# A decoder layer on one core: the second MLP product in seven half-depth products, with operand sums made by transfers, and a reordered SSD loop

## The chip, the cores and the metric

The kernel runs as one program on 1 core of a Trainium2 chip. Its metric is the device time of one execution in microseconds. Matrix products run on TensorE (PE; PEld is its weight load), element work on VectorE (DVE), ScalarE (ACT) and GpSimd (POOL). SyncE (SP), ACT and POOL also issue transfers (DMA) between DRAM and the on-chip memory SBUF; products are accumulated in PSUM banks.

## What is computed

One layer on 1024 tokens of width 1024, in float32: a norm, a wide input projection, three mixers side by side (GLA, windowed attention, Mamba-2 SSD), a gated merge, an output projection, and then the MLP. The two places that the change touches are, cut from the reference:

```python
def _ssd(z, xbc, dt_raw, ...):                       # 32 heads in 4 groups, chunks of 128 tokens
    a_cs = jnp.cumsum(dtc * A, axis=2)
    seg = a_cs[:, :, :, None] - a_cs[:, :, None, :]
    Lmat = jnp.exp(jnp.where(causal, seg, -inf))     # decay between two tokens of a chunk, per head
    CB = jnp.einsum('bnlgd,bnsgd->bnlsg', Cc, Bc)
    y_diag = jnp.einsum('bnlsgh,bnsghp->bnlghp', CB[..., None] * Lmat, xdt)
    ...                                              # plus the state carried from chunk to chunk
    y = (y_diag + y_off + D_skip * xc) * silu(z)     # then a norm over the 512 columns of a group

h2 = _rmsnorm(x, norm_mlp)
x = x + (jnp.square(jax.nn.relu(h2 @ w_mlp_in)) @ w_mlp_out) * vmask     # 1024 -> 4096 -> 1024
return _rmsnorm(x, final_norm)
```

## The kernel before

Every float32 operand of a large product is split into a high part `hi` (a ScalarE cast) and a rest `lo` (a VectorE subtraction), and a product is three matmuls: hi by hi, hi by lo, lo by hi. The first part of the kernel holds the normed input in SBUF and makes the projection beside the mixers; work that no mixer waits for (the `z` and gate projections, lines 158 to 160 and 186 to 188) is put between the mixers' steps to fill TensorE. The order of the instructions on each engine is made when the program is built, from priorities (`tc.high_priority`) and the scheduler's own idea of durations; at run time each engine takes its list in order, and an instruction that waits holds up all behind it on its engine.

**SSD (lines 557 to 673).** For each of 4 groups, 8 chunks c of 128 tokens. A transfer from SP (L632) spreads the chunk's running sums of 8 heads over all partitions into the 128x1024 tile `ab` (two buffers), another (L634) loads `zt`. POOL subtracts the per-token sums (L635), DVE clamps at 0 (L636), ACT takes the exponential (L637), DVE multiplies by `cb` (L638). Eight small matmuls, one per head, give `psD` (L643), one gives `psY` from the carried state (L646), one the next state (L657). DVE and POOL assemble y (L648 to L662), ACT sums its squares into `zt` (L664), POOL makes the reciprocal root by a power (L88), ACT scales y (L666), and TensorE transposes y in four pieces at once (L669), followed by a copy (L671) and a store. So the transposes of a chunk stand in TensorE's list before the next chunk's `psD` or close to it.

**MLP.** The first product already runs as seven products per unit of 256 hidden columns (`unit_a` to `unit_e`, 16 units); a unit leaves four 128x512 tiles of the squared ReLU in DRAM (`hid_d`), named here by K half and token half: x11, x21, x12, x22. The second product (lines 1039 to 1080) runs over 16 blocks of 256 rows of K: two loads of hidden values and two of weights (512 KB each, from SP), splits (L152, L153 and L127, L128), then for 8 token tiles and 2 column halves six matmuls of 512 columns (L847 to L849) and one addition into the residual `x2b` (L1062). In the last block the final norm and the output stores follow each token tile. Pools that matter: 22 tiles `o` of 128x1024 float32 (split operands), 2 pairs `w_hi`, `w_lo`, 3 tiles `w_raw`, 4 tiles `h2`, 8 PSUM banks.

## Time and profile before

| | us |
|---|---|
| median of 3 runs (2729.49 to 2734.89) | 2734.1 |
| the profiled execution's own time | 2735.99 |
| its span in the trace | 2734.4 |
| SSD loops of the four groups, in the span | 954 to 1025, 1134 to 1212, 1335 to 1408, 1515 to 1589 |
| second MLP product, in the span | 2371 to 2724 |

The profile is of one execution. A row of a group gives the line of the code, the engine, the operation with output and input tiles, how often it ran, then the busy time in us and the mean of one in ns, and after the second bar the idle time of the engine just before it and what ended that. "PEclk" is the share of full speed that TensorE's clock was granted. A matmul on float32 (not split) operands is recorded twice.

### The profile page before, as it was taken

To read this page: it belongs to the slowest core of one execution; us is meant where nothing else is said; L and a number is where in the kernel's file an instruction comes from. 1 tells how busy PE (TensorE), PEld (TensorE's weight loads), DVE (VectorE), ACT (ScalarE), POOL (GpSimd) and SP (SyncE) were. 2 spreads that over 40 slices of the span, in tenths; PEclk is the share of its full clock that TensorE was granted. 3 is DMA by queue.
4 is the path that set the end of the run, shared out by engine and by line. 5 is a ranking of instruction groups with operands and counts; after the bars stand their busy time and mean duration, and the time that the engine had idled before them with its cause. 6 is when DMAs were issued, how large, how long until landed. Compare 5 with 4: busy or idle time off the path is not lost.

```text
span 2734.4 us, 36866 instructions
## 1 busy us (share of the span) xinstructions
PE 2634.5 (96%) x14565; PEld 2284.4 (84%) x14565; DVE 1451.0 (53%) x2463; ACT 1049.2 (38%) x1915; POOL 386.2 (14%) x326
## 2 busy tenths in 40 slices
PE   8999999999999989989989899999998999999998
PEld 7998988888888979879879678888996888888887
DVE  5333323256664573653655653444437666676666
ACT  6423433246664454353454343323234333321212
POOL 1000000011221150340340410322200000000001
PEclk9999999999999999989989999999998999999999
DMA  4211112212223152252251464433322333533231
GB/s 141 63 40 54 47 47 62 77 52 76 61 68 93 51 123 74 67 122 74 76 133 46 122 224 150 150 113 110 124 78 81 108 108 113 204 124 96 93 100 62
DMA packets 223951, 260.48 MB, mean 95 GB/s; under 512 B 14382, under 2 KB 176484, under 8 KB 223780
## 3 DMA queue, kind: packets, MB, share of 16 engines
q1 hardware_dynamic: 178820, 207.74, 25.7%
q10 hardware_dynamic: 44960, 50.40, 5.2%
q8 instruction: 114, 1.87, 0.3%
q14 instruction: 57, 0.47, 0.1%
HBM read 195.05 MB, written 63.05 MB: 94 GB/s over the span
## 4 chain that ended last, share of the span: by engine, by line
PE 80%; DVE 5%; DMA 5%; ACT 4%; issue 3%; POOL 2%; SPq 0%; ACTq 0%; POOLq 0%; DVEq 0%
PE acc_ps L158 8%; PE acc_ps L159 8%; PE acc_ps L160 8%; PE pp_ps L778 8%; PE pp_ps L849 5%; PE pp_ps L847 5%; PE pp_ps L848 5%; PE pp_ps L781 4%; DMA ab<-acs_d 4%; PE pp_ps L933 3%; PE pp_ps L935 3%; PE pp_ps L936 3%; PE acc_ps L186 3%; PE acc_ps L188 3%; PE acc_ps L187 3%
## 5 line engine op out<-in xcount | busy, mean ns | idle before, releaser
L158 PE MATMUL acc_ps<-hh,w_hi 128*128 128x512 f32 (+6 forms) x1320 | 472.0, 358 | 3.3 <-ACT rt L352 1.7
L159 PE MATMUL acc_ps<-hl,w_hi 128*128 128x512 f32 (+6 forms) x1320 | 475.1, 360 | 0.0
L160 PE MATMUL acc_ps<-hh,w_lo 128*128 128x512 f32 (+6 forms) x1320 | 470.6, 356 | 0.0
L186 PE MATMUL acc_ps<-w_hi,hh 128*128 128x256 f32 x1056 | 308.4, 292 | 1.9 <-ACT zst L199 1.3
L187 PE MATMUL acc_ps<-w_lo,hh 128*128 128x256 f32 x1056 | 309.0, 293 | 0.0
L188 PE MATMUL acc_ps<-w_hi,hl 128*128 128x256 f32 x1056 | 308.1, 293 | 0.0
L128 DVE TENSOR_TENSOR w_lo<-w_raw,w_hi 128x1024 fp32r<-128x1024 f32 (+1 forms) x156 | 200.5, 1307 | 155.4 <-ACT w_hi L127 155.3
L158 PEld LDWEIGHTS acc_ps<-hh,w_hi 128*128 128x128 f32 (+1 forms) x1320 | 247.6, 188 | 32.8 <-ACT rt L352 2.6
L847 PE MATMUL pp_ps<-w_hi,o 128*128 128x512 f32 (+1 forms) x768 | 270.7, 354 | 1.4 <-ACT w_hi L127 1.4
L849 PE MATMUL pp_ps<-w_hi,o 128*128 128x512 f32 (+1 forms) x768 | 271.5, 354 | 0.1
L848 PE MATMUL pp_ps<-w_lo,o 128*128 128x512 f32 (+1 forms) x768 | 271.4, 354 | 0.0
L159 PEld LDWEIGHTS acc_ps<-hl,w_hi 128*128 128x128 f32 (+1 forms) x1320 | 247.8, 188 | 26.6 <-issue 2.4
L160 PEld LDWEIGHTS acc_ps<-hh,w_lo 128*128 128x128 f32 (+1 forms) x1320 | 248.0, 188 | 26.0 <-issue 2.4
L127 ACT CAST w_hi<-w_raw 128x1024 fp32r<-128x1024 f32 (+1 forms) x156 | 154.7, 1040 | 274.7 <-PE pp_ps L849 122.2
L188 PEld LDWEIGHTS acc_ps<-w_hi,hl 128*128 128x128 f32 x1056 | 201.3, 191 | 11.2 <-issue 10.5
L186 PEld LDWEIGHTS acc_ps<-w_hi,hh 128*128 128x128 f32 x1056 | 201.6, 191 | 9.2 <-issue 4.7
L187 PEld LDWEIGHTS acc_ps<-w_lo,hh 128*128 128x128 f32 x1056 | 201.3, 191 | 5.3 <-issue 4.4
L781 PE MATMUL pp_ps<-o,w_hi 128*128 128x512 f32 x512 | 198.9, 389 | 0.0
L778 PE MATMUL pp_ps<-o,w_hi 128*128 128x512 f32 x512 | 197.1, 389 | 1.2 <-ACT o L152 1.2
L1062 DVE TENSOR_TENSOR x2b<-pp_ps,x2b 128x512 f32<-128x512 f32 x256 | 169.3, 685 | 45.4 <-PE pp_ps L849 43.5
L933 PE MATMUL pp_ps<-o,w_hi 128*128 128x512 f32 x448 | 177.4, 398 | 9.3 <-ACT o L152 9.2
L935 PE MATMUL pp_ps<-o,w_hi 128*128 128x512 f32 x448 | 177.2, 395 | 2.1 <-DVE o L153 2.1
(298 smaller groups left out, 4657.1 us busy)
## 6 DMA issues: line engine op xcount, KB each, us to landing
w_raw<-in_w_in_dram SPq DMA_DIRECT2D x80, 512.0 KB, 3.7
ab<-acs_d SPq DMA_DIRECT2D x32, 512.0 KB, 9.2
g<-gate SPq DMA_DIRECT2D x64, 256.0 KB, 4.0
w_raw<-in_w_mlp_in_dram SPq DMA_DIRECT2D x32, 512.0 KB, 4.1
hid<-hid ACTq DMA_DIRECT2D x64, 256.0 KB, 3.3
w_raw<-hid SPq DMA_DIRECT2D x32, 512.0 KB, 4.4
w_raw<-in_w_mlp_out_dram SPq DMA_DIRECT2D x32, 512.0 KB
gate<-gst ACTq DMA_DIRECT2D x48, 256.0 KB, 2.0
```

The source lines that it names most:

```text
L158: nc.tensor.matmul(ps, lhsT=lh, rhs=rh, start=(i == 0), stop=False)
L159: nc.tensor.matmul(ps, lhsT=lh, rhs=rl, start=False, stop=False)
L160: nc.tensor.matmul(ps, lhsT=ll, rhs=rh, start=False, stop=(i == n - 1))
L186: nc.tensor.matmul(o, lhsT=h_h, rhs=whi[:, k, off:off + width], start=(k == 0), stop=False)
L187: nc.tensor.matmul(o, lhsT=h_h, rhs=wlo[:, k, off:off + width], start=False, stop=False)
L188: nc.tensor.matmul(o, lhsT=h_l, rhs=whi[:, k, off:off + width], start=False, stop=(k == KD - 1))
L778: nc.tensor.matmul(ps[b], lhsT=lh, rhs=xs[b][:, 0, :], start=(st and k == 0), stop=(sp_ and k == n - 1))
L781: nc.tensor.matmul(ps[b], lhsT=lh, rhs=xs[b][:, 1, :], start=False, stop=False)
L847: nc.tensor.matmul(ps, lhsT=x[:, 0], rhs=rh, start=(i == 0), stop=False)
L848: nc.tensor.matmul(ps, lhsT=x[:, 0], rhs=rl, start=False, stop=False)
L849: nc.tensor.matmul(ps, lhsT=x[:, 1], rhs=rh, start=False, stop=(i == n - 1))
L933: nc.tensor.matmul(ps, lhsT=h[:, kk, :], rhs=x[:, 0, :], start=(first and kk == 0), stop=False, skip_group_check=True)
```

## The change

It has three parts.

**SSD decay.** The POOL subtraction and the DVE clamp on 128x1024 are replaced by eight DVE instructions on 128x128, one per head, that subtract a per-partition scalar and clamp in one step.

**SSD transposes.** The four transposes of y, the copy and the store move into a function `y_out`, called one chunk later: they are issued behind the last `psD` matmul of the next chunk.

**Second MLP product.** The 16 blocks of 256 rows become 4 chunks q of 1024 rows, each cut in two K halves; tokens and output columns are halved too. Seven products of 4 token tiles by 512 columns and 512 rows of K (each 48 matmuls: 4 tiles, 4 K steps of 128, 3 split parts) replace the eight of the plain form. With a for weights (a{column half}{K half}) they are, in order: P1 x11·a11, P2 x21·a12, P3 (x22-x12)·(a11+a21), P4 (x22-x12+x11)·(a11+a21+a22), P5 (x22-x12+x11-x21)·a22, P6 (x11-x12)·(a22+a21), P7 x22·(a11+a21+a22+a12). The sums are made in place by transfers that add (`accum_op`, issued from POOL) onto a raw tile from which the product before was split; the subtractions need negated hidden values, so the first MLP product stores n21 and n12, each negated by ACT. Per chunk there are 14 plain loads of 512 KB from SP and 16 adding transfers of 512 KB from POOL. A common term is kept in four tiles `rr` and added into the residual at the end.

```diff
-                    nc.gpsimd.tensor_tensor(ab, ab, up(tms[:, c, 32 + 8 * g:40 + 8 * g], 2, [P, 8, P]), sub)
-                    nc.vector.tensor_scalar(ab, ab, 0.0, None, op0=amin)
+                    for h in range(8):
+                        nc.vector.tensor_scalar(ab[:, h, :], ab[:, h, :], tms[:, c, 32 + 8 * g + h:33 + 8 * g + h], 0.0,
+                                                op0=sub, op1=amin)
...
+                    if c:
+                        with tc.issue_after(mm.ins):
+                            y_out(c - 1, yn)
...
-                    ps = bank(bk, "tr", 2)
-                    for i in range(4):
-                        nc.tensor.transpose(out=ps[:, i * P:(i + 1) * P], in_=y[:, i * P:(i + 1) * P], identity=ident)
...
+                    yn = y
+                y_out(NT - 1, yn)
...
+        def neg(g):
+            n = g_tile()
+            nc.scalar.activation(n, g, AF.Copy, scale=-1.0)
+            return n
...
-        NB = 16
-        for blk in range(NB):
...
+            def add(self, i, *names):
+                for nm in names:
+                    if self.t[i] is None:
+                        self.t[i] = half_raw(self.pool)
+                        nc.sync.dma_start(self.t[i], self.src(nm, i))
+                    else:
+                        nc.gpsimd.dma_start(self.t[i], self.src(nm, i), accum_op=add)
+                return self.t[i]
...
+        def w_op(chain, *names):
+            hi = wp.tile([P, 2048], F32R, tag="whi", name="w_hi")
+            lo = wp.tile([P, 2048], F32R, tag="wlo", name="w_lo")
+            tiles = []
+            for i in range(2):
+                r = chain.add(i, *names)
+                h, l = (t[:, i * 1024:(i + 1) * 1024].rearrange("p (v c) -> p v c", v=2) for t in (hi, lo))
+                nc.scalar.copy(h, r)
+                nc.vector.tensor_tensor(l, r, h.bitcast(F32), sub)
...
+        for q in range(NQ):
+            hs_, ws_ = hid_src(q), w2_src(q)
+            xa, wa = Chain(op, hs_), Chain(op, ws_)
+            a = four()
+            first_r = (lambda t, ps: nc.scalar.copy(rr[t], ps)) if q == 0 else evict("r", add)
+            product(a, x_op(xa, "x11"), w_op(wa, "a11"), True, True, first_r)
+            product(a, x_op(Chain(tp, hs_), "x21"), w_op(Chain(None, ws_), "a12"), False, True, evict("c11", add))
+            xb = Chain(op, hs_)
+            b = four()
+            product(b, x_op(xb, "x22", "n12"), w_op(wa, "a21"), True, True, evict("c22", sub))
+            a = four()
+            product(a, x_op(xb, "x11"), w_op(wa, "a22"), True, True, evict("r", sub))
+            wb = Chain(None, ws_)
+            last = q == NQ - 1
...
+            product(b, x_op(xb, "n21"), w_op(wb, "a22"), False, True, c21_done)
+            c = four()
...
+            product(c, x_op(xa, "n12"), w_op(wb, "a21"), True, True, c22_done)
+            product(c, x_op(Chain(tp, hs_), "x22"), w_op(wa, "a12"), False, True, c12_done)
```

The order changes with it. TensorE in the SSD loop of the first group, at the fourth chunk's `psD` (before) and the fourth's (after): L643 and L654 are `psD`, L669 and L632 the transposes of y, L186 to L189 filling work. Before:

```order
L669 MATMUL ps_tr<-ident,y 128x128 x4
L643 MATMUL ps_y<-xd,ab 128x64 x8
L646 MATMUL ps_y<-S,CF 128x512
L657 MATMUL ps_y<-xe,BT 128x512
L187 MATMUL acc_ps<-w_lo,hh_173 128x256
```

After:

```order
L654 MATMUL ps_y<-xd,ab 128x64 x3
L632 MATMUL ps_tr<-ident,y 128x128 x4
L654 MATMUL ps_y<-xd,ab 128x64 x5
L660 MATMUL ps_y<-S,CF 128x512
L671 MATMUL ps_y<-xe,BT 128x512
L189 MATMUL acc_ps<-w_hi,hl_190 128x256
```

The transposes, of a y that is one chunk older, now stand inside or behind `psD`, not ahead of it. POOL in the same loop, where L635 is the decay subtraction, L88 the power for the norm of y, and L655 (L669 after), L659 (L673) and L648 (L662) the products with the state and D. Before:

```order
L635 TENSOR_TENSOR ab<-ab,tms 128x1024
L88 TENSOR_TENSOR yrs<-ms,mhalf 128x1
L655 TENSOR_TENSOR xe<-xT,tms 128x512
L635 TENSOR_TENSOR ab<-ab,tms 128x1024
L659 TENSOR_TENSOR S<-S,decb 128x512
L648 TENSOR_TENSOR y<-xT,db 128x512
L88 TENSOR_TENSOR yrs<-ms,mhalf 128x1
```

After:

```order
L669 TENSOR_TENSOR xe<-xT,tms 128x512
L88 TENSOR_TENSOR yrs<-ms,mhalf 128x1
L673 TENSOR_TENSOR S<-S,decb 128x512
L662 TENSOR_TENSOR y<-xT,db 128x512
L88 TENSOR_TENSOR yrs<-ms,mhalf 128x1
```

The subtraction that stood ahead of each power is gone. On SP in the same loop the transfers for `ab` and `zt` alternated strictly; now the `ab` of one chunk ahead goes out before the `zt`. In the second MLP product of before, SP issues all transfers; a stretch of two blocks:

```order
L1044 DMA w_raw<-hid_137 128x1024
L1044 DMA w_raw<-hid_138 128x1024
L1051 DMA w_raw<-in_w_mlp_out_dram 128x1024 x2
L1044 DMA w_raw<-hid_139 128x1024
L1044 DMA w_raw<-hid_140 128x1024
```

In the changed kernel POOL's list of the second chunk q=1 is this (hid_x and hid_n are stored and negated hidden values, two numbers for the two K quarters; `o` rows of weights belong to the chain of P1, P3, P4 and P7, the `w_raw` ones to that of P5 and P6):

```order
L1105 DMA o<-hid_n_144 128x2x512
L1105 DMA o<-in_w_mlp_out_dram 128x2x512 x2
L1105 DMA o<-hid_x_141 128x2x512
L1105 DMA o<-hid_n_149 128x2x512
L1105 DMA o<-hid_x_146 128x2x512
L1105 DMA o<-hid_n_145 128x2x512
L1105 DMA o<-hid_n_150 128x2x512
L1105 DMA o<-in_w_mlp_out_dram 128x2x512 x4
L1105 DMA w_raw<-in_w_mlp_out_dram 128x2x512 x2
```

The adding transfers are one list, and the third sum of weights (first two of the x4) stands behind the sums of P5's hidden operand.

## Rows read from the trace of the kernel before

**Rows 1.** The page: span, and busy time, share and instructions of each engine.

```profile
span 2734.4 us, 36866 instructions
PE 2634.5 (96%) x14565; PEld 2284.4 (84%) x14565; DVE 1451.0 (53%) x2463; ACT 1049.2 (38%) x1915; POOL 386.2 (14%) x326
```

**Rows 2.** Stretches: the four SSD loops; from:to, length, busy (count), PEclk, DMA share, GB/s.

```profile
953.90:1025.00 71.10, 59.51 (x377) 50.08 (x376) 51.87 (x63) 35.60 (x51) 36.07 (x28) 0.92 0.51 116
1133.90:1211.50 77.60, 67.28 (x352) 53.12 (x350) 52.23 (x65) 32.99 (x49) 42.43 (x31) 0.86 0.53 120
1335.30:1408.00 72.70, 62.60 (x385) 51.86 (x385) 50.71 (x63) 35.60 (x51) 36.24 (x28) 0.88 0.49 115
1514.90:1589.00 74.10, 64.95 (x317) 48.96 (x316) 51.07 (x63) 24.28 (x40) 36.65 (x30) 0.95 0.42 114
```

**Rows 3.** Line 643 in each loop: count, ns min/median/max, first and last start.

```profile
L643 PE MATMUL ps_y<-xd,ab x128: 217/275/443, 953.9 to 1023.1; 128*128 128x64 f32 x128
L643 PE MATMUL ps_y<-xd,ab x128: 217/275/423, 1133.9 to 1209.5; 128*128 128x64 f32 x128
L643 PE MATMUL ps_y<-xd,ab x128: 217/275/447, 1335.3 to 1406.0; 128*128 128x64 f32 x128
L643 PE MATMUL ps_y<-xd,ab x128: 217/275/421, 1514.9 to 1587.4; 128*128 128x64 f32 x128
```

**Rows 4.** Waits in the SSD stretch: who <- for whom: total us, times, longest.

```profile
PE ps_tr L669 <- ACT y L666: 39.3, 20, 4.9
PE ps_y L643 <- DVE ab L638: 11.0, 8, 2.7
...
SPq L634 <- ACT zt L664: 158.9, 22, 14.7
...
POOL ab L635 <- DMA ab<-acs_d: 97.2, 27, 9.2
...
ACT y L666 <- POOL yrs L88: 61.1, 23, 6.5
```

**Rows 5.** Groups by form, of POOL, DVE and ACT: the decay steps and DVE's small forms.

```profile
L635 POOL TENSOR_TENSOR ab<-ab,tms 128x1024 f32<-128x1024 f32 x32 | 63.4, 1980 | 139.9 <-DMA ab<-acs_d 127.6 <-PE acc_ps L188 8.5 <-PE ps_y L657 3.7
...
L638 DVE TENSOR_TENSOR ab<-ab,cb 128x1024 f32<-128x1024 f32 x32 | 43.3, 1363 | 13.0 <-ACT ab L637 13.0
L636 DVE TENSOR_SCALAR ab<-ab 128x1024 f32<-128x1024 f32 x32 | 35.6, 1112 | 85.1 <-POOL ab L635 85.1
L240 DVE TENSOR_SCALAR h<-xt,rs 128x1024 f32<-128x1024 f32 x8 | 6.0, 752 | 3.7 <-POOL rs L88 3.7
L86 DVE TENSOR_SCALAR ms<-yss 128x1 f32<-128x1 f32 x32 | 4.7, 148 | 15.1 <-ACT zt L664 14.9
...
L637 ACT ACTIVATE ab<-ab 128x1024 f32<-128x1024 f32 x32 | 33.8, 1057 | 42.6 <-DVE ab L636 42.5
```

**Rows 6.** Transfers by line: KB each, median us from issue to landing.

```profile
ab<-acs_d SPq DMA_DIRECT2D x32, 512.0 KB, 9.2
...
w_raw<-hid SPq DMA_DIRECT2D x32, 512.0 KB, 4.4
...
x2b<-x_d SPq DMA_DIRECT2D x8, 512.0 KB, 7.2
```

**Rows 7.** TensorE in order of time in the second MLP product: start, length; 15 matmuls.

```profile
2499.68 0.39 PE L849 MATMUL pp_ps<-w_hi,o 128*128 128x512 f32 x1
...
2502.85 0.39 PE L848 MATMUL pp_ps<-w_lo,o 128*128 128x512 f32 x1
```

**Rows 8.** Stretches: the second MLP product, and 20 us near its start.

```profile
2374.00:2716.00 342.00, 342.00 (x1511) 283.18 (x1510) 237.65 (x352) 70.66 (x107) 4.89 (x6) 1.00 0.32 107
2380.00:2400.00 20.00, 20.00 (x90) 16.57 (x89) 15.82 (x24) 5.04 (x8) 0.00 (x0) 1.00 0.83 315
```

**Rows 9.** Groups of the stretch 2235 to 2734: DVE's additions and weight splits.

```profile
L1062 DVE TENSOR_TENSOR x2b<-pp_ps,x2b 128x512 f32<-128x512 f32 x256 | 169.3, 685 | 45.4 <-PE pp_ps L849 43.5 <-PE pp_ps L936 1.5
L128 DVE TENSOR_TENSOR w_lo<-w_raw,w_hi 128x1024 fp32r<-128x1024 f32 x32 | 39.0, 1220 | 6.2 <-ACT w_hi L127 6.2
```

More of the change, by code (lines that the diff above doesn't have):

```diff
@@ L627, in ssd, with y_out @@
                 zfill(8 * FZ[g], g + 1)
+            def y_out(c, y):
+                ps = bank(bk, "tr", 2)
+                for i in range(4):
+                    nc.tensor.transpose(out=ps[:, i * P:(i + 1) * P], in_=y[:, i * P:(i + 1) * P], identity=ident)
+                st = ep.tile([P, CH], F32, tag="st", name="yst", bufs=2)
+                nc.scalar.copy(st, ps)
+                nc.scalar.dma_start(ossd[g].rearrange("(i p) t -> p i t", p=P)[:, :, c * P:(c + 1) * P],
+                                    st.rearrange("p (i t) -> p i t", i=4))
             with tc.high_priority(offset=HPE):
@@ new lines, in hid_src, with w2_src, src, x_op @@
+        def hid_src(q):
+            return lambda nm, i: hid_d[2 * q + i, nm].rearrange("(v p) t -> p v t", p=P)
+        def w2_src(q):
+            def src(nm, i):
+                r0 = q * 1024 + i * 512
+                v = w_mlp_out[0][r0:r0 + 512, :].rearrange("(v j p) d -> p j v d", j=2, p=P)
+                fh, dh = {"a11": (0, 0), "a12": (1, 0), "a21": (0, 1), "a22": (1, 1)}[nm]
+                return v[:, fh, :, dh * 512:(dh + 1) * 512]
+            return src
+        def x_op(chain, *names):
+            tiles = []
+            for i in range(2):
+                r = chain.add(i, *names)
+                hi, lo = hl_tile(), hl_tile()
+                nc.scalar.copy(hi, r)
+                nc.vector.tensor_tensor(lo, r, hi.bitcast(F32), sub)
+                for v in range(2):
+                    tiles.append((hi[:, v, :], lo[:, v, :]))
+            return tiles
@@ new lines, in product @@
+        def product(ps, xo, wo, first, last, done):
+            for t in range(4):
+                ts = slice(t * P, (t + 1) * P)
+                for kk in range(4):
+                    (xh, xl), (wh, wl) = xo[kk], wo[kk]
+                    nc.tensor.matmul(ps[t], lhsT=xh[:, ts], rhs=wh, start=(first and kk == 0), stop=False,
+                                     skip_group_check=True)
+                    nc.tensor.matmul(ps[t], lhsT=xh[:, ts], rhs=wl, start=False, stop=False, skip_group_check=True)
+                    nc.tensor.matmul(ps[t], lhsT=xl[:, ts], rhs=wh, start=False, stop=(last and kk == 3),
+                                     skip_group_check=True)
+                done(t, ps[t])
```

131 lines of the change are left out of this document (79 added, 52 removed).

## The prediction

> **What bounds the kernel now.** I read the page first: TensorE is busy for 2634.5 of 2734.4 us, no other engine above 53% [rows 1]. So time is gained by taking work from TensorE, or its stalls, and the next question is where it stalls. Stretches by stage answer that. In the second MLP product it never stops: 342.00 of 342.00 us at a granted clock of 1.00, with one matmul of 512 columns every (2502.85 - 2499.68)/14 = 0.2264 us [rows 7, 8]. In the four SSD loops it is idle for 11.6 + 10.3 + 10.1 + 9.2 = 41 of 295.5 us, and the clock mean is 0.86 to 0.95; (1 - clock) times length adds up to another 29 us [rows 2]. Without both, its work in a chunk is (254.3 - 29)/29.5 = 7.6 us. What a chunk takes in fact comes from the first and last start of `psD` in each loop: less 8 x 0.217 = 1.7 us for the heads of the last chunk, over 7 steps, 9.6, 10.6, 9.9 and 10.1, mean 10.0 us [rows 3].
>
> The waits say why [rows 4]: TensorE's largest is its transposes waiting for ACT's scaled y (39.3 us, 1.4 a step), ACT waits for POOL's power (61.1), and POOL stands in its subtraction waiting for the `ab` transfer (97.2 us in 27 waits, 3.6 each) with the power queued behind it. A second ring is the `ab` buffer: transfer 9.2, POOL 1.98, DVE 1.11, ACT 1.06, DVE 1.36, `psD` 1.7, together 16.4 us for two buffers, 8.2 a chunk [rows 5, 6]. So 1.8 of the 10.0 us is queueing.
>
> **The SSD loop, part by part.** Removed: POOL's 1.98 and DVE's 1.11 us. Added: eight DVE instructions on 128x128, a size that the trace doesn't have in this form. A scalar-pointer form takes 0.752 us on 1024 columns, a small one 0.148 on one [rows 5]; on the line between, 128 columns take 0.22, eight 1.8 us. The low end is 8 x 0.148 = 1.2; for the high end, DVE's clamp beside POOL's work takes 1.112 against 0.752 for the same size elsewhere, 1.48 times as much, so 2.6. I take 1.8, since POOL has less to do afterwards. The `ab` ring falls to 9.2 + 1.8 + 1.06 + 1.36 + 1.7 = 15.1, or 7.6 a chunk: 0.65 less. DVE's own work is 205.9/29.5 = 7.0 a chunk [rows 2] and becomes 7.0 - 1.1 + 1.8 = 7.7.
>
> Moved: the transposes, and with them the copy and the store on ACT, stand a chunk later, when their y has been ready for most of a chunk, so the 1.4 us wait should go; late next is `psD` itself on `ab` (11.0 us now). POOL no longer waits for a transfer; the wait passes to DVE's subtraction, with y's additions and the weight splits queued behind it. On SP the next `ab` now goes out ahead of `zt`, which waited for ACT's squares 22 times at 7.2 us [rows 4]: a help I don't price by itself.
>
> A step thus gains between 0.65 (the ring alone) and 0.65 + 1.4. Over 28 steps that is 18 to 57 us; a loss is the second rival's. I take 34 (8.8 us a step), a little below the middle, as part of the transposes' wait is the ring seen from another engine. The floors, 7.6, 7.6 and 7.7 us, lie below 8.8.
>
> **The second MLP product.** The matmuls fall from 16 x 8 x 2 x 6 = 1536 to 4 x 7 x 48 = 1344: 192 x 0.2264 = **43.5 us off** an engine that is never idle there. A product takes 48 x 0.2264 = 10.87 us. Beside it DVE has four splits and four additions, 4 x 1.220 + 4 x 0.685 = 7.6 us [rows 9], 70% of the time, as large a share as now (237.65/342, rows 8). The sums into `rr`'s targets in the last chunk, 12 x 0.685 = 8.2 us, fit in the 3 x 3.3 us that DVE has left in P5 to P7. ACT's 32 negations in the first MLP product, at about half of 1.06 us some 17 us, lie on an engine that is 38% busy [rows 1]: nothing, at most 17.
>
> New are the adding transfers, of which the trace shows none. A plain 512 KB transfer occupies all engines for 0.524 MB at 107/0.32 = 334 GB/s, 1.57 us [rows 8]. An addition also reads its target: between 1.57 and, read twice, 3.14 us. A chunk then needs 14 x 1.57 + 16 x (1.57 to 3.14) = 47 to 72 us of transfer time in 7 x 10.87 = 76.1 us of matmuls: hidden, with little to spare at the high end. Latency: weights are split one product ahead (two `w_hi` pairs), so from one split of a chain to the next there are two products, 21.7 us, less DVE's 7.6: a sum may take some 14 us; a plain load lands in 4.4 us, 7.2 in a crowd [rows 6]. But POOL's list is one queue, and the weight sum for P4 stands behind the hidden sums for P5, which wait for P4's own split. I take 2 us a chunk in the last three chunks, 6 in all; ends 0, and for slow transfers the third rival.
>
> At the start nothing is ahead. After the first product ends, SP has 18 plain loads to bring (8 of them the residual) and POOL 8 sums before P4 can run: 18 x 1.57 + 8 x (1.57 to 3.14) = 41 to 53 us against three products, 32.6. That is 8 to 21 us of stall; I take 15, TensorE's slower clock after a stall included. Before, 315 GB/s at a share of 0.83 covered that place [rows 8].
>
> Sum: 2736.0 (profiled execution, span 2734.4) - 34 - 43.5 + 6 + 15 = 2679.5; the median of the runs is 1.9 lower, so **2678 us**.
>
> **Rivals.** *A, everything hidden:* the loop gains 57, the product loses only 8 at its start: 2734.1 - 57 - 35.5 = 2642. For it: the transfers are busy for only 0.32 of the time now [rows 8]. Against: 8.0 us a step would be within 0.4 of three floors at once.
>
> *B, DVE takes POOL's place:* DVE waits in order for `ab` as POOL did. If it keeps 2.3 us a step of waiting, 7.7 + 2.3 = 10.0 and the loop gains nothing: 2734.1 - 22.5 = 2712. If it inherits all of POOL's 3.6, a step takes 11.3, 36 us more in all: 2748. It decides from 10.8 us a step (28 x 0.8 = 22) on. For it: the order puts the subtraction ahead of y's additions. Against: POOL's 1.98 us between landing and DVE is gone. The Trainium skill (SBUF — State Buffer, Who interferes with whom) has a rule against this part: a `tensor_scalar` of DVE in its two-port mode and a GpSimd instruction shut each other out for a whole instruction. By it eight small instructions could each meet one of POOL's; POOL has three of half L635's size, so an estimate of 3 x 0.99 = 3.0 us more for DVE, 10.7 a step and 2731 us; the 1.112 against 0.752 us for one size agrees with the rule in kind.
>
> *C, the adding transfers are the bound, slower than before:* the product lasts 4 x (22.0 + 16t) + 15 us, if one addition occupies the transfer engines for t. It is bound by them from t = 3.4, and the whole kernel is slower than before when 4 x (22.0 + 16t) + 15 - 348 exceeds 34, from t = 4.4 us. At 6 us, midway between 3.14 and the 9.2 of the slowest 512 KB transfer here (`ab`, rows 6): 487 - 348 - 34 = 105 us more, 2839. For it: no row has such a transfer, and 16 a chunk are many. Against: 4.4 is 2.8 times a plain one. The Trainium skill (DMA: Bandwidth & Descriptors, Issuing engines are not separate DMA queues) says that transfers from POOL run on the same 16 engines as SP's, so a second issuing engine adds no rate; by it the two terms of the bracket add up, as here.
>
> That the matmuls aren't saved is no rival: the count is fixed by the loops.
>
> **How the numbers follow.** Forecast 0.50, alone 2660 to 2700. A 0.15, B 0.17, C 0.13, and 0.05 that the new waits eat most of the 43.5 us while the loop gains (about 2700). A measurement of this kernel tells 0.2%, 5.5 us, from no change. Faster: 0.50 + 0.15 + 0.05 + 0.09 of B = 0.79. Same: 0.05 of B. Slower: 0.03 of B + 0.13 = 0.16. The range 2640 to 2745 leaves out the better half of A, C and a little of B, under 0.2.
>
> **What would show it.** Starts of `psD` 8.8 us apart, the transposes' wait gone and POOL never waiting for `ab`; 10.0 or more with DVE waiting for it is B. In the second product, 1344 matmuls, stalls of about 15 us in the first chunk and 2 in each later one; a transfer share near 1.0 with TensorE waiting for splits of summed tiles is C. The forecast is wrong if an addition takes over 3.4 us of the engines, or if POOL's order makes each chunk wait.

## The result: 0.5% slower, and where the time went

| | us |
|---|---|
| kernel before, median of 5 runs (2729.05 to 2734.89) | 2732.8 |
| changed kernel, median of 5 runs (2744.15 to 2748.39) | 2745.4 |
| ratio, with its 95% interval | 1.0051 (1.0036 to 1.0065) |
| profiled execution of the changed kernel; its span | 2748.4; 2746.7 |

The forecast was 2678 us with a range up to 2745, and faster. The page of the changed kernel, in the same form as [rows 1]:

```profile
span 2746.7 us, 36564 instructions
PE 2630.9 (96%) x14373; PEld 2255.5 (82%) x14373; DVE 1419.9 (52%) x2567; ACT 1117.5 (41%) x1971; POOL 402.3 (15%) x358
```

The 192 matmuls are gone (14565 to 14373), yet TensorE is as busy as before: 2630.9 against 2634.5 us. So look at the stages, by first and last start of their matmuls. Kernel before: the branch products (L778), the first MLP product (L933), the second (L849, which also serves the output projection, so only its last start counts here); columns are count, ns min/median/max, first and last start:

```profile
L778 PE MATMUL pp_ps<-o,w_hi x512: 389/389/499, 1595.3 to 1944.1; 128*128 128x512 f32 x171
L933 PE MATMUL pp_ps<-o,w_hi x448: 389/389/796, 2041.0 to 2381.1; 128*128 128x512 f32 x150
L849 PE MATMUL pp_ps<-w_hi,o x768: 282/389/389, 1945.3 to 2724.1; 128*128 128x512 f32 x128, 128*128 128x256 f32 x64
```

The same code in the changed kernel (L787, L942; the second MLP product is L1151):

```profile
L787 PE MATMUL pp_ps<-o,w_hi x512: 387/398/481, 1587.8 to 1945.1; 128*128 128x512 f32 x171
L942 PE MATMUL pp_ps<-o,w_hi x448: 389/392/796, 2041.0 to 2387.6; 128*128 128x512 f32 x150
L1151 PE MATMUL pp_ps<-w_hi,o x448: 387/393/628, 2378.1 to 2737.9; 128*128 128x512 f32 x150
```

| stretch of the span | before | after | difference |
|---|---|---|---|
| up to the branch products | 1595.3 | 1587.8 | -7.5 |
| branch products (code not touched) | 348.8 | 357.3 | +8.5 |
| output projection, norm | 96.9 | 95.9 | -1.0 |
| first MLP product (same matmuls) | 340.1 | 346.6 | +6.5 |
| second MLP product, to its last matmul | 343.0 | 350.3 | +7.3 |
| end | 10.3 | 8.8 | -1.5 |
| span | 2734.4 | 2746.7 | +12.3 |

Three things need a cause. The SSD part brought 7.5 us, not 34. Two stages whose matmuls did not change are 15 us longer. And the second MLP product, with an eighth of its matmuls gone, takes 7.3 us more.

**The second MLP product stands still.** Stretches of the changed kernel in the form of [rows 8], which showed 342.00 busy of 342.00 us at a clock of 1.00 and a transfer share of 0.32:

```profile
2374.00:2716.00 342.00, 313.35 (x1287) 249.24 (x1286) 200.38 (x230) 115.58 (x128) 77.06 (x64) 0.95 0.84 191
2380.00:2400.00 20.00, 13.80 (x60) 10.85 (x58) 7.38 (x9) 6.02 (x9) 1.10 (x1) 0.96 1.07 341
2400.00:2420.00 20.00, 14.25 (x48) 11.04 (x48) 8.90 (x10) 4.93 (x5) 4.35 (x4) 0.76 1.04 301
2420.00:2440.00 20.00, 13.74 (x40) 10.58 (x41) 3.65 (x4) 3.04 (x3) 6.53 (x6) 0.69 0.74 124
2500.00:2520.00 20.00, 15.46 (x54) 11.47 (x53) 11.11 (x13) 7.58 (x8) 6.05 (x5) 0.83 0.60 98
2580.00:2600.00 20.00, 17.47 (x68) 13.36 (x67) 8.06 (x9) 5.99 (x6) 3.66 (x4) 0.91 0.61 122
```

Idle is 342 - 313.35 = 28.7 us, and the lower clock costs more, 0.05 x 342 = 17 us if all of it had fallen into busy time. Added up over the starts of the matmuls, what the gaps have over 0.2325 us comes to 43 us, so about 14 us are the clock. Idle time comes in the first 60 us and then again about every 80 us, once in a chunk; after the stops of the first three chunks the granted clock drops (0.76 and 0.69, 0.83, 0.91). The waits in that stretch (2376 to 2740), the chain of them from TensorE backwards; who waits for whom, total, times, longest:

```profile
POOL o L1105 <- DVE o L1125: 103.2, 15, 12.1
ACT o L1124 <- DMA o<-hid_n: 80.6, 14, 11.5
...
PE pp_ps L1148 <- ACT o L1124: 18.2, 3, 8.5
```

TensorE waits for ACT's copy of a summed tile, ACT waits for the adding transfer (`o<-hid_n`), and POOL, which has to issue it, waits for DVE's split of something else. POOL in order of time in the second chunk, with the idle time before each entry:

```profile
2481.31 1.20 POOL L1105 DMA_DIRECT2D o<-hid_n  x1 [13.70 <-PE pp_ps L1151]
2482.04 2.95 POOL L1105 DMA_DIRECT2D o<-in_w_mlp_out_dram  x2
2489.61 1.20 POOL L1105 DMA_DIRECT2D o<-hid_x  x1 [4.63 <-DVE o L1125]
2490.34 1.71 POOL L1105 DMA_DIRECT2D o<-hid_n  x1
```

These are the first rows of POOL's list that stand in the section on the change (that list leaves out the two hidden sums for P6, which went out at 2464.32 and 2466.40). The first `hid_n` is the first half of P3's sum. Its second half is the fourth row, at 2490.34, 9 us later, because one entry between them, `hid_x`, belongs to P4 and has to wait until P3's first half has landed and been split. ACT sees the second half at 2501.18:

```profile
2487.00 1.05 ACT L1124 CAST o<-o 128x1024 fp32r<-128x1024 f32 x1 [9.27 <-DMA o<-hid_n]
...
2501.18 1.99 ACT L1124 CAST o<-o 128x1024 fp32r<-128x1024 f32 x2 [11.22 <-DMA o<-hid_n]
```

**The untouched matmuls are slower.** 1536 matmuls in the branch products take 348.8/1536 = 0.2271 us each before and 357.3/1536 = 0.2326 after, at a granted clock of 1.00 in both. This was in no term of the prediction. One line of the change that looks like bookkeeping moves tiles: `sq`, two floats for a row's squares, gets eight buffers instead of four. Each buffer takes 32 B in the allocation, and what is allocated behind, the tiles `o` of the whole second part among them, moves up by 128 B; the weight tiles, allocated ahead, stay. Before, `o` and the weight tiles both start 96 B past a multiple of 256 B; after, `o` starts 224 B past one.

**The SSD loop.** `psD` in each loop, as in [rows 3], and the waits of the SSD stretch, as in [rows 4]:

```profile
L654 PE MATMUL ps_y<-xd,ab x128: 217/275/422, 955.7 to 1020.9; 128*128 128x64 f32 x128
L654 PE MATMUL ps_y<-xd,ab x128: 217/275/474, 1130.4 to 1205.7; 128*128 128x64 f32 x128
L654 PE MATMUL ps_y<-xd,ab x128: 217/275/443, 1328.0 to 1394.1; 128*128 128x64 f32 x128
L654 PE MATMUL ps_y<-xd,ab x128: 217/275/422, 1505.2 to 1578.0; 128*128 128x64 f32 x128
```

```profile
DVE ab L646 <- DMA ab<-acs_d: 81.6, 26, 6.2
...
PE ps_tr L632 <- ACT y L680: 22.1, 11, 6.0
```

The steps are 9.1, 10.5, 9.2 and 10.2 us, mean 9.7 against 10.0; 8.8 was forecast. The transposes' wait fell from 39.3 us in 20 to 22.1 in 11, and DVE now waits for the `ab` transfer nearly as long as POOL did (97.2 us in 27).

### The profile page after: what moved, and what is told of

The parts are those of the page before. It is cut to its first block, busy times and chain, and to the rows that moved or that the text cites. A ratio compares the mean times of both kernels' runs of the same rounds, so it can differ in the third digit from the quotient of the medians.

```text
span 2746.7 us, 36564 instructions
## 1 busy us (share of the span) xinstructions
PE 2630.9 (96%) x14373; PEld 2255.5 (82%) x14373; DVE 1419.9 (52%) x2567; ACT 1117.5 (41%) x1971; POOL 402.3 (15%) x358
## 5 line engine op out<-in xcount | busy, mean ns | idle before, releaser
L189 PE MATMUL acc_ps<-w_hi,hl 128*128 128x256 f32 x1056 | 304.0, 289 | 0.0
L129 DVE TENSOR_TENSOR w_lo<-w_raw,w_hi 128x1024 fp32r<-128x1024 f32 (+1 forms) x124 | 159.7, 1315 | 145.3 <-ACT w_hi L128 144.0
L1148 PE MATMUL pp_ps<-w_hi,o 128*128 128x512 f32 x448 | 183.0, 410 | 28.4 <-ACT o L1124 18.2
L189 PEld LDWEIGHTS acc_ps<-w_hi,hl 128*128 128x128 f32 x1056 | 198.4, 188 | 9.7 <-issue 8.9
L787 PE MATMUL pp_ps<-o,w_hi 128*128 128x512 f32 x512 | 201.4, 398 | 0.0
L790 PE MATMUL pp_ps<-o,w_hi 128*128 128x512 f32 x512 | 200.4, 392 | 0.0
L128 ACT CAST w_hi<-w_raw 128x1024 fp32r<-128x1024 f32 (+1 forms) x124 | 122.7, 1036 | 179.0 <-PE acc_ps L160 69.2
L942 PE MATMUL pp_ps<-o,w_hi 128*128 128x512 f32 x448 | 179.3, 402 | 9.5 <-ACT o L153 9.2
L1150 PE MATMUL pp_ps<-w_lo,o 128*128 128x512 f32 x448 | 182.6, 408 | 0.2
L944 PE MATMUL pp_ps<-o,w_hi 128*128 128x512 f32 x448 | 179.3, 400 | 2.4 <-DVE o L154 2.4
L945 PE MATMUL pp_ps<-o,w_lo 128*128 128x512 f32 x448 | 178.5, 399 | 0.0
L1151 PE MATMUL pp_ps<-w_hi,o 128*128 128x512 f32 x448 | 176.4, 399 | 0.0
```

The costliest lines, as they stand in the source:

```text
L189: nc.tensor.matmul(o, lhsT=h_l, rhs=whi[:, k, off:off + width], start=False, stop=(k == KD - 1))
L787: nc.tensor.matmul(ps[b], lhsT=lh, rhs=xs[b][:, 0, :], start=(st and k == 0), stop=(sp_ and k == n - 1))
L790: nc.tensor.matmul(ps[b], lhsT=lh, rhs=xs[b][:, 1, :], start=False, stop=False)
L942: nc.tensor.matmul(ps, lhsT=h[:, kk, :], rhs=x[:, 0, :], start=(first and kk == 0), stop=False, skip_group_check=True)
L1148: nc.tensor.matmul(ps[t], lhsT=xh[:, ts], rhs=wh, start=(first and kk == 0), stop=False, skip_group_check=True)
L1150: nc.tensor.matmul(ps[t], lhsT=xh[:, ts], rhs=wl, start=False, stop=False, skip_group_check=True)
```

## Experiments

Times are medians; each ratio is against the kernel before on the same chip, with its 95% interval.

### e1: the operands back in their old place

```diff
-                sqs[t] = sm.tile([P, 2], F32, tag="sq", name="sq", bufs=8)
+                sqs[t] = sm.tile([P, 2], F32, tag="sq", name="sq")
```

> The changed kernel with four buffers for the tile sq of the final norm, as in the kernel before, where the change has eight. Each buffer takes 32 B, so the split operands o and all tiles of the second part lie 128 B lower again, where they lay before the change. Theory of operand placement: in the profile of the changed kernel the 128x512 matmuls on o follow each other at 0.2325 us at a granted clock of 1.00, before the change at 0.2267 us, in code that the change doesn't touch; 4272 less 192 of them times 5.9 ns is 24 us, so about 2721 us, 0.4% faster than before, cadence 0.2267 us from the branch stage on. Rival (the slower cadence comes from the chip, from more DMA traffic or from the order of the work): about 2745 us and 0.2325 us as in the changed kernel.

2734.7 us, 0.9994 (0.9985 to 1.0003): the same as before. Against the kernel before, each on its own chip, the changed kernel is 12.7 us slower and e1 0.6 us faster: the placement cost 13 us, where 24 were expected. (Matmuls of 512 columns on these tiles are 1536 + 1344 + 1536 = 4416 in the kernel before, not the 4272 of the expectation.) Its rows:

```profile
L787 PE MATMUL pp_ps<-o,w_hi x512: 387/389/504, 1587.3 to 1936.3; 128*128 128x512 f32 x171
L942 PE MATMUL pp_ps<-o,w_hi x448: 389/389/796, 2033.2 to 2374.6; 128*128 128x512 f32 x150
L1151 PE MATMUL pp_ps<-w_hi,o x448: 387/389/628, 2363.8 to 2724.1; 128*128 128x512 f32 x150
```

The branch products take 349.0 us and the first MLP product 341.4, as before the change: 13.5 us less than in the changed kernel, and the span is 13.7 less. The cadence theory holds for them. The second MLP product takes 349.5 us against 350.3, though its matmuls are faster: it waits for its operands, so a faster matmul only waits sooner.

### e2, e9, e10: the kernel before with its tiles moved

```diff
-                            sq = sm.tile([P, 2], F32, tag="sq", name="sq")
+                            sq = sm.tile([P, 2], F32, tag="sq", name="sq", bufs=8)
```

(e9 has 6 and e10 has 12 in place of 8.)

> The kernel before with eight buffers for sq instead of four and nothing else: the same work in the same order, with the tiles of the second part 128 B higher. Theory of operand placement: 4272 matmuls of 128x512 on these tiles at 5.9 ns more each, 25 us, less about 1 us on the 768 of 128x256 that were faster in the changed kernel (0.1187 against 0.1200 us): about 2757 us, 0.9% slower than before. Rival (cadence depends on something else in the change): 2733 us, the same as before.

> The kernel before with six buffers for sq: the tiles of the second part 64 B higher. With 128 B more (eight buffers) it took 2759 us against 2735, with 0.2325 us for a 128x512 matmul on o in place of 0.2267. If any distance other than that of before (o tiles and weight tiles both 96 B past a multiple of 256 B) is slow: about 2757 to 2759 us. If only a shift by 128 B is slow, or the slow cadence grows with the shift: 2735 us or about 2747 us.

> The kernel before with twelve buffers for sq: the tiles of the second part 256 B higher. If what counts is where a tile lies within 256 B: 2735 us and 0.2267 us, as before. If any move of these tiles against the weight tiles costs, or the eight buffers themselves: about 2759 us and 0.2325 us.

| moved by | us | ratio | one of the branch products |
|---|---|---|---|
| 64 B (e9) | 2754.0 | 1.0065 (1.0052 to 1.0078) | 352.1/1536 = 0.2292 us |
| 128 B (e2) | 2759.0 | 1.0094 (1.0080 to 1.0108) | 358.5/1536 = 0.2334 us |
| 256 B (e10) | 2735.0 | 1.0003 (0.9994 to 1.0012) | 348.9/1536 = 0.2271 us |

The stretch 2420 to 2680, inside the second MLP product: length, TensorE's busy time and count, clock, transfer share, GB/s. The kernel before, then e2:

```profile
2420.00:2680.00 260.00, 260.00 (x1149) 1.00 0.30 94
```

```profile
2420.00:2680.00 260.00, 260.00 (x1121) 1.00 0.31 99
```

Both never idle, at the full clock, with the same transfers, and 28 matmuls fewer fit into 260 us: 0.2263 against 0.2319 us each. Nothing but the place of the tiles differs. As far as these three shifts go, what counts is where a tile lies within 256 B; the rival that any move costs, or the eight buffers themselves, falls with e10. The 64 B step was not foreseen. In the branch products it costs less than 128 B, but in the second MLP product it costs as much (260/1116 = 0.2330 us), so the two stages differ; the same stretch of e9:

```profile
2420.00:2680.00 260.00, 260.00 (x1116) 1.00 0.29 94
```

The 256 B step is shown; whether the tiles' own place matters or the distance from the weight tiles is not, since only `o` was moved.

### e3, e7, e8: the SSD part, whole and in its two halves

e3 is the kernel before with all of the change's SSD part, e7 with the decay alone, e8 with the later transposes alone. The edit of e7:

```diff
-                    nc.gpsimd.tensor_tensor(ab, ab, up(tms[:, c, 32 + 8 * g:40 + 8 * g], 2, [P, 8, P]), sub)
-                    nc.vector.tensor_scalar(ab, ab, 0.0, None, op0=amin)
+                    for h in range(8):
+                        nc.vector.tensor_scalar(ab[:, h, :], ab[:, h, :], tms[:, c, 32 + 8 * g + h:33 + 8 * g + h], 0.0,
+                                                op0=sub, op1=amin)
```

> The kernel before with the SSD part of the change alone (decay per head on VectorE, output transposes one step later); the MLP as before. The last SSD transpose of the changed kernel starts 7.4 us earlier than before, the last filler matmul too, so this should gain 7 to 9 us: about 2725 us. The prediction on record had 34 us for this part (2700 us). A rival would be that the branch stage gives it back (its first loads are queued behind): 2733 us.

> The kernel before with the decay per head on VectorE and nothing else of the change; output transposes where they were. The prediction on record gave the whole SSD part 34 us and asked for a step of 8.8 us instead of 10.0; the whole part measured 4 us (2731.5 against 2735.3), its steps 9.0, 10.3, 9.25 and 9.9 us in the four groups. If the decay alone does it (POOL's 1.9 us out of the chain, VectorE's small operations 2.2 us in it): 2731 us. If VectorE has taken POOL's place in the chain and the later transposes made the gain: 2735 us or a little slower.

> The kernel before with the output transposes and their copy one step later and nothing else; decay on POOL and VectorE as before. TensorE's wait for y before the transposes was 39 us in 20 before the change and 22 us in 11 after. If that is what was gained: 2731 us, and the run before shows 2735. If the wait only moves to the next product of the step (psD, behind VectorE): 2735 us.

e3: 2731.5 us, 0.9984 (0.9975 to 0.9992), between the two outcomes expected (2725 and 2733). e7: 2727.8 us, 0.9976 (0.9965 to 0.9986). e8: 2734.5 us, 0.9998 (0.9989 to 1.0006). So the decay brings 4 to 6 us, the later transposes nothing; with both the gain is no larger than with the decay alone.

The later transposes bring nothing because they are not later. In the trace of the kernel before, each of the 28 groups of transposes that have a next chunk starts behind the last `psD` of that chunk already, 6.9 us behind it in the mean, because ACT has scaled y only 16 us after y's own `psD` (means over the chunks, from the start of the last `psD` matmul). So to ask for the place behind the next `psD` asks for nothing new: `psD` and the transposes stand on TensorE in the same order in e8 as in the kernel before, and in the same order in e3 as in e7. The wait for ACT's y that was to go (39.3 us in 20 before) is still there in e8, and it is the decay that shortens it (e7). The two rows, e8 and then e7:

```profile
PE ps_tr L631 <- ACT y L678: 40.5, 18, 5.0
```

```profile
PE ps_tr L670 <- ACT y L667: 26.6, 10, 6.9
```

### e4: the MLP part alone

The kernel before with the MLP part of the change, and four buffers for `sq`.

> The kernel before with the MLP part of the change alone and four buffers for sq, so that the operands lie as before. By the prediction's terms -43.5 +6 +15 = -22.5 us: about 2710 us. By the changed kernel's trace the product stage has 28 to 30 us of idle TensorE and about 17 us of lower clock, so that next to nothing of the 43.5 us stays: about 2728 us (2721 us for the whole change with its operands in the old place, plus the 7 us of the SSD part). If the two parts were not additive, it would lie outside 2720 to 2732.

2739.0 us, 1.0015 (1.0006 to 1.0024), outside the 2720 to 2732 that were expected if the parts add up; but that range rested on 2721 us for e1, which measured 2734.7. The two parts do add up: +3.7 us here and -3.8 in e3 give 0, and e1, which has both, measured -0.6. So the second MLP product by itself gains nothing, though 43.5 us of matmuls are gone.

### e11: without the adding transfers

```diff
-                    else:
-                        nc.gpsimd.dma_start(self.t[i], self.src(nm, i), accum_op=add)
```

(from e1; the sums are left out, so the operands are the first load of each chain)

> The changed kernel with four sq buffers, and the 64 adding transfers left out: every chain keeps its first load, so the operands of products 3 to 7 are not the sums. All splits, matmuls and evictions stay, and 33.6 MB less is moved. If the adding transfers make all idle time of the stage but for what SP's queue does at its start: 31.9 us of idle and about 14 us of lower clock go, but for some 8 to 12 at the start, so 2695 to 2705 us against 2735. If the splits or the operand buffers make it: 2720 us or more.

2681.1 us, 0.9807 (0.9793 to 0.9821), better than any of the outcomes expected. A stretch at the start of the product:

```profile
2380.00:2400.00 20.00, 19.89 (x88) 16.17 (x87) 14.84 (x17) 11.82 (x13) 0.00 (x0) 1.00 0.26 99
```

TensorE is busy for 19.89 of 20 us, at the full clock. Against the kernel before, e11 is 53.6 us faster and e1 0.6 us, so the adding transfers cost 53 us, the start included: without them SP's 18 loads, the residual's among them, stop nothing.

### e5, e6: the same transfers in another order

e5 asks for both halves of P3's sum before anything of P4. e6 also asks for them ahead of P2's operands, and moves the eight loads of the residual behind them on SP's queue (`issue_after` keeps them there).

```diff
             xb = Chain(op, hs_)
+            for i in range(2):
+                xb.add(i, "x22")
+            for i in range(2):
+                xb.add(i, "n12")
             b = four()
-            product(b, x_op(xb, "x22", "n12"), w_op(wa, "a21"), True, True, evict("c22", sub))
+            product(b, x_op(xb), w_op(wa, "a21"), True, True, evict("c22", sub))
```

> The changed kernel with four sq buffers (operands in the old place), and in the MLP-out chunk the two halves of the sum x22 + n12 are asked for together, ahead of anything of product 4, so that on GpSimd's queue the second half's adding transfer stands before product 4's first one; in the changed kernel it stands behind it, and that one waits until the first half has landed, been added to and been split. The work is the same. Theory (the queue order makes the stall): the third product's operands come 8 to 10 us earlier in each of four chunks; the idle TensorE time at the places of the stall (6.9 us at 2480, 5.4 at 2560, 4.2 at 2640 to 2680, some 9 of 15.9 at 2380 to 2420) goes, with the half clock behind it, 5 to 10 us: about 2705 us against 2735 of the same kernel without it (2700 to 2715). Rival (the transfers are late because the 16 DMA engines are full, share 0.9 to 1.07 in the first 40 us and 0.6 to 1.0 later, whatever the order): 2730 to 2735 us, and the same idle time in the same places.

> As the run before, with the loads of x22 asked for ahead of product 2's operands, and the eight loads of the residual x2 (4 MB) put behind them on SP's queue instead of in front. If the start of the stage waits for SP's queue (the residual's loads at 2354 to 2381 us, and the x22 loads only at 2386 and 2390), the rest of the first stall goes too, 6 to 8 us and some 4 us of clock: about 2695 us. If the start is bound by the bytes that are needed at once, it is as the run before. If the residual now comes late for the first eviction (about 20 us into the stage), it is slower than the run before by that wait, up to 10 us.

e5: 2715.9 us, 0.9928 (0.9916 to 0.9940), 18 us less than e1 by their ratios; 2705 us were expected, 2715 at most. POOL in the second chunk of e5, to be read beside the POOL rows of the changed kernel above:

```profile
2467.38 1.20 POOL L1105 DMA_DIRECT2D o<-hid_n  x1 [11.40 <-DMA o<-hid_x]
...
2468.83 2.22 POOL L1105 DMA_DIRECT2D o<-hid_n  x1
...
2475.87 1.20 POOL L1105 DMA_DIRECT2D o<-hid_x  x1 [3.58 <-DVE o L1125]
```

The second half of P3's sum now goes out 1.5 us after the first, not 9. With the same bytes the stops of the later chunks get small. The stop of the second chunk in e1, from which e5 was made, and then in e5:

```profile
2480.00:2500.00 20.00, 13.15 (x46) 10.00 (x45) 5.38 (x6) 3.68 (x4) 3.64 (x3) 0.83 0.62 127
```

```profile
2480.00:2500.00 20.00, 17.86 (x71) 13.97 (x70) 13.90 (x17) 8.32 (x9) 5.87 (x5) 0.91 0.82 164
```

So the order made them, not the bytes, and the rival that the 16 engines are full falls for the later chunks. e6: 2706.1 us, 0.9897 (0.9881 to 0.9912), another 10 us, against some 10 to 12 expected (2695 us was expected, on top of e5's 2705). Of the 53 us of the adding transfers, 28 were order; 25 are left, mostly at the start. e6's stretches (its profiled execution, 2711.6 us, is the slowest of its five):

```profile
2360.00:2400.00 40.00, 34.54 (x144) 27.60 (x142) 17.56 (x20) 11.69 (x15) 7.96 (x7) 0.96 0.98 299
2400.00:2440.00 40.00, 31.64 (x112) 24.06 (x113) 17.84 (x18) 14.92 (x15) 9.69 (x8) 0.85 1.03 226
2440.00:2700.00 260.00, 257.64 (x1133) 212.95 (x1132) 181.57 (x218) 101.71 (x123) 69.69 (x60) 1.00 0.82 184
```

14 us idle in the first 80 us, at a transfer share of about 1.0, and 2.4 us in all the rest.

The traces also give the time lost to idle and lower clock together: the sum of what the gaps between starts of matmuls have over the cadence (0.2325 us in the changed kernel, 0.2267 in the others), for the first quarter of the product's matmuls, which is the first chunk, and for the other three chunks:

| us lost | first chunk | other three |
|---|---|---|
| taken in the prediction | 15 | 6 |
| changed kernel | 26.1 | 17.1 |
| e1 | 26.1 | 25.9 |
| e5 | 23.0 | 6.0 |
| e6 | 23.3 | 2.6 |
| e11 | 0.4 | 0.0 |

The order of the sums cost the later chunks 20 us and the first one 3. What is left sits in the first chunk.

### e12: a version that beats both

e6 with the output transposes where they were before the change.

> A version meant to beat both kernels: the second MLP product of the change with the adding transfers and the loads in the order of e6, four sq buffers, the decay per head, and the output transposes where they were before the change. By the single runs: 2706 us of e6, less the difference of the SSD part with and without later transposes (2731.5 against 2727.8, both by their own comparison, 2 to 4 us): 2703 us, 1.1% faster than before.

2707.2 us, 0.9900 (0.9887 to 0.9914): 1.0% faster than before, no better than e6, where 2703 were expected. By their ratios it is 1.5% faster than the changed kernel. Taking the transposes back, expected to bring 2 to 4 us, shows nothing here, as it should if the move changed no order.

### e13 to e16: is it the `ab` transfer that paces the SSD loop?

e13 and e15 give `ab` a third buffer (and `yst` one less, for room), e14 and e16 give `zt` a third; e13 and e14 with the decay of e7, e15 and e16 with the decay of the kernel before. The edit of e13 and e15:

```diff
-                    ab = ep.tile([P, 8, P], F32, tag="ab", name="ab", bufs=2)
+                    ab = ep.tile([P, 8, P], F32, tag="ab", name="ab", bufs=3)
...
-                    st = ep.tile([P, CH], F32, tag="st", name="yst", bufs=2)
+                    st = ep.tile([P, CH], F32, tag="st", name="yst", bufs=1)
```

> The decay-only kernel of e7 (2728 us) with three buffers for ab instead of two (one less for yst, to make room). In e7's trace VectorE waits 84 us in 25 of the SSD steps for the load of ab, and the load's issue on SP's queue waits 97.5 us in 22 steps for the products psD that free its buffer two steps back. If the load of ab paces the step, and not VectorE's eight operations: the wait goes, the steps come down from 9.8 us by up to 2 us, and TensorE's idle time in the four loops (some 30 us) falls by 10 to 20 us: 2708 to 2718 us. If VectorE's chain paces it, or the z loads on the same queue (e14): 2726 to 2730 us.

> The decay-only kernel of e7 with three buffers for zt instead of two. The load of zt stands ahead of the next step's ab on SP's queue and waits 151 us in 27 steps for ScalarE to have read zt two steps back. If that queue place makes ab late: 2708 to 2718 us. If ab's own buffer (e13) or VectorE paces the step: 2726 to 2730 us.

> The kernel before (decay as before) with three buffers for ab and one for yst. In the trace of before, the load's issue waits 29 us in 8 steps for its buffer's psD and POOL waits 97 us in 27 steps for the load. If the load of ab paces the step in the kernel before too, this gains about what e13 gains over e7 (10 to 20 us): 2715 to 2725 us. If there the chain POOL, VectorE, ScalarE, VectorE paces it: 2733 to 2736 us.

> The kernel before with three buffers for zt. In its trace the zt load on SP's queue waits 159 us in 22 steps for ScalarE. If that queue place makes ab late in the kernel before: 2715 to 2725 us; if not: 2733 to 2736 us.

e13: 2734.4 us, 0.9993 (0.9983 to 1.0003). e14: 2735.2 us, 0.9995 (0.9986 to 1.0004). e15: 2745.0 us, 1.0030 (1.0019 to 1.0042). e16: 2740.8 us, 1.0015 (1.0004 to 1.0025). None gains; all are slower than their starting point by 5 to 9 us, and slower than any outcome expected for them. The third buffer for `ab` took only a part of the wait for its transfer away, DVE's from 84.2 us (e7) to 66.3 (e13) and POOL's from 97.2 to 87.8 (e15); the third for `zt` left it at 84.1 (e14) and 119.3 (e16). What a loop without that wait would take is not shown. Yet e15's loops did get shorter; `psD` in each:

```profile
L643 PE MATMUL ps_y<-xd,ab x128: 217/275/475, 959.2 to 1024.6; 128*128 128x64 f32 x128
L643 PE MATMUL ps_y<-xd,ab x128: 217/275/423, 1140.5 to 1210.9; 128*128 128x64 f32 x128
L643 PE MATMUL ps_y<-xd,ab x128: 217/275/423, 1338.6 to 1403.1; 128*128 128x64 f32 x128
L643 PE MATMUL ps_y<-xd,ab x128: 217/275/421, 1518.2 to 1591.3; 128*128 128x64 f32 x128
```

Steps of 9.1, 9.8, 9.0 and 10.2 us, mean 9.5 against 10.0 [rows 3], but the first loop starts 5.3 us later and the last ends 3.9 us later. A shorter step is not a shorter kernel here. The four loops of e15 are 15 us shorter, the stretches between them 13 us longer; in the loops TensorE works for 239.6 us against 254.3 before and is idle for 41 us as before. So the loops hold less of the work that fills TensorE between the steps, and that work stands outside them. Why the first loop starts later with the third buffer stays open.

## Why the prediction was wrong

**The removed matmuls: right.** 1536 became 1344, and without the adding transfers (e11) the kernel is 53.6 us faster than before: 43.5 for the matmuls, about 4 for the SSD part, the other 6 without a term. The 53 us of the adding transfers and the 13 of the place of the tiles turn that into the 12.7 us by which the changed kernel is slower.

**The stalls of the second product: the step that failed most.** The sum had 21 us, 15 at the start and 2 in each later chunk. The changed kernel lost 43 us, 26 in its first chunk and 17 in the others, and with the operands in their old place 52 (e1, 26 and 26); without the adding transfers next to nothing is lost (e11). Their size was judged well enough. The changed kernel shows a median of 7.9 and 7.6 us from issue to landing, inside the 14 us that the prediction allowed for a sum. POOL's queue (the first row: packets, MB, share of the 16 engines) took 49.9% of the 16 engines for the 396 us from 2350 to 2746; over 64 transfers that is 3.09 us each, the high end of the 1.57 to 3.14 that the prediction gave:

```profile
q0 software_dynamic: 17408, 33.56, 49.9%
o<-hid_n POOLq DMA_DIRECT2D x24, 512.0 KB, 7.9
o<-in_w_mlp_out_dram POOLq DMA_DIRECT2D x24, 512.0 KB, 7.6
```

What failed for the later chunks is the reading of POOL's list. The prediction said that the weight sum for P4 stands behind sums of P5, and took 2 us a chunk for it. The harmful row stands five lines higher in the same list: P4's first hidden sum (`hid_x_141`) ahead of P3's second (`hid_n_149`). With it, the two halves of P3's sum are made one after the other, each with its own landing and split, and a sum takes 20 us (2481.31 to 2501.18), not 8. The allowance of 14 us was exceeded by the order, not by the transfer. Undoing that one order (e5) took the later chunks from 26 us lost to 6.0, which is the prediction's own term, and gave 18 us back; earlier loads of x22 and later ones of the residual gave another 10 (e6, not told apart).

At the start the term was too small: 15 us taken, 8 to 21 allowed, 26 lost, and 23 lost even with the order put right (in e6 14 of them idle, the rest at the lower clock). At 3.09 us an addition the prediction's own account gives 18 x 1.57 + 8 x 3.09 - 32.6 = 20 us, so most of what is left agrees with transfers that cannot be there in time. That sum fits, but it is argued: no run made the same sums with fewer bytes. The lower clock after the stops, some 14 us over the whole stage of the changed kernel, had a term only at the start.

**A price in none of its terms: the place of the tiles.** 128 B made 4416 matmuls of the kernel before slower by 24 us in all (e2), and cost the changed kernel 13 us net (e1), because the second product could not use faster matmuls. With its tiles in the old place the changed kernel would have come out inside the range, at 2734.7 us, and the loop and the stalls would have been as wrong as they are: that would have been luck. The prediction took the 0.2264 us of [rows 7] for a property of the instruction; it was one of that instruction on these addresses. The Trainium skill (TensorE: Matmul & The Clock Gate, Back-to-back issue gap) gives the gap of isolated matmuls at full clock as N / 2.4 + 2.5 ns, 216 ns for 512 columns, and a sustained spacing of about 131 ns, and has no dependence on where operands lie. No run here shows 216 or 131: the rows show 226 to 227, or 229 to 233 with the tiles moved, and the measurement decides.

**The SSD part: 34 us forecast, 4 measured (e3).** Its steps can be judged one by one. The eight small operations were sized well: DVE's group by form in the SSD stretch shows 62.2/240 = 0.26 us each, 2.1 a step against 1.8 taken.

```profile
L646 DVE TENSOR_SCALAR ab<-ab,tms 128x128 f32<-128x128 f32 x240 | 62.2, 329 | 81.6 <-DMA ab<-acs_d 81.6
```

The mechanism of rival B is there: DVE inherited POOL's wait, 81.6 us against 97.2. B's milder form, 10.0 us a step and nothing gained, came nearest of all (9.7 us a step, 4 us gained); its 36 us lost did not come.

The step that failed is the gain of 1.2 us a step, 0.65 from the `ab` ring and the rest from the transposes' wait. The transposes were read as standing ahead of the next `psD`, with a y that would be ready for most of a chunk after the move. In the kernel before they stand behind that `psD` already and wait for a y that comes 6.3 us after it in the mean, so the move moved nothing (e8); their wait fell with the decay alone, from 39.3 to 26.6 us in e7, as with both (22.1). Of the ring's 0.65 the steps show 0.3 (10.0 to 9.7), as DVE still waits for the transfer.

The floor behind that gain was too low as well. The prediction took 41 us of idle and 29 us of lower clock out of TensorE's time to get 7.6 us a chunk, and so had room for 8.8. The changed kernel's stretches over the same part of the loops:

```profile
953.00:1022.60 69.60, 63.23 (x400) 52.03 (x399) 51.51 (x113) 38.86 (x54) 20.70 (x22) 0.90 0.47 123
1130.40:1207.40 77.00, 65.21 (x344) 52.16 (x342) 53.74 (x114) 33.31 (x49) 27.23 (x24) 0.84 0.51 120
1328.00:1395.80 67.80, 60.73 (x371) 50.72 (x370) 48.35 (x106) 37.86 (x51) 26.61 (x21) 0.87 0.47 116
1505.20:1579.70 74.50, 65.55 (x310) 49.46 (x308) 49.79 (x105) 24.42 (x40) 25.68 (x24) 0.91 0.41 113
```

TensorE is busy for 254.7 of 288.9 us, as long as before (254.3), and the clock did not come back (0.84 to 0.91, against 0.86 to 0.95). At the clock that the loop gets, TensorE needs 8.6 us a step, so the most that could be gained was the 41 us of idle, and 34 would have needed nearly all of it. Idle fell from 41 to 34 us, about the 7.5 us by which the branch products start earlier. Why the first and third loop gain (9.6 to 9.1, 9.9 to 9.2) and the second and fourth don't stays open.

**The rivals.** C, the adding transfers as the bound, came closest in place (TensorE waiting for splits of summed tiles, a transfer share of 0.84 in the stage), but in the later chunks by another mechanism: not t, the time that one addition occupies the engines, which measured 3.09 us and lies below C's 3.4, but the order on one queue; e5 and e6 move the same bytes and win 28 us. In the first chunk, where nothing is loaded ahead, C is near the truth. Its statement that POOL's transfers share SP's 16 engines, as the Trainium skill (DMA: Bandwidth & Descriptors, Issuing engines are not separate DMA queues) has it, agrees with the first 40 us, where both queues together fill them (share 1.07 and 1.04 at 341 and 301 GB/s). By the prediction's own chances its range leaves out a little over 0.2 (0.075 of A, 0.13 of C and a little of B), not under it.

## What to carry to other kernels

When transfers with operands of their own are issued from one in-order queue, go down the list entry by entry: for each, what it waits for, and who is waiting for the next one; half of one operand behind a step that depends on its other half costs a whole round trip. Before you price a move in an engine's order, look in the trace where the instruction stands now and when its operand is ready: a place asked for that it has already is worth nothing. A floor for an engine has to be taken at the clock that the stage gets, unless the change shows why the clock would rise. And compare the cadence of instructions that the change does not touch: if it moved, look at what the change did to the allocation, and try the old addresses before explaining the rest.

## What the runs showed of the hardware

- A 128x512 matmul on split float32 operands starts every 0.2263 to 0.2271 us with its tiles in one place and every 0.2319 to 0.2334 us with one of them 128 B further, at a granted clock of 1.00; 256 B further it is as fast as at first, and 64 B further takes 0.2292 us in the branch products and 0.2330 in the second MLP product. Over the second part of this kernel that is 24 us, 0.9%.
- The slower cadence costs nothing where TensorE waits for operands anyway: the second MLP product of the changed kernel took 350.3 us with the one and 349.5 us with the other.
- An adding transfer of 512 KB from POOL takes 3.09 us of the 16 engines (64 of them, 49.9% of 396 us), about twice the 1.57 us of a plain one, and lands in 7.6 to 7.9 us (median) in a stage whose transfer engines are 84% busy; the plain loads of operands beside it take 5.7 to 8.0 and, without the adding transfers, 3.7 to 5.0 (e11).
